# One-bank PSUM tiles in rotation for the last layer's FFN, and the norm product behind its first three blocks

## The chip, the core and the metric

The kernel runs on one core of a Trainium2 chip. TensorE (PE in the profile) does the matrix products and writes them into PSUM, 8 banks of 512 f32 in each of 128 partitions. VectorE (DVE), ScalarE (ACT) and GpSimd (POOL) work on tiles, and SyncE (SP) issues transfers. Each engine takes its instructions in the order of its program. The metric is the device time of one execution in microseconds. The kernel before takes 1583.85 us, the median of three runs (1581.45 to 1584.41).

## The reference, cut to what matters

One step of a decoder of two layers, for 512 prompt rows and 8 x 8 sample rows together (576 columns in the kernel, two halves of 288). The first layer mixes with attention, the second with a state-space layer and a GLU projection. After each mixer comes a feed-forward network (FFN) on the normed rows:

```
def rmsnorm(x, g):
    y = xf * lax.rsqrt(jnp.mean(xf * xf, axis=-1, keepdims=True) + RMS_EPS)
    return (y * g.astype(jnp.float32)).astype(x.dtype)
def swiglu(h, w_gate, w_up, w_down):
    return (jax.nn.silu(h @ w_gate) * (h @ w_up)) @ w_down
...
        h2 = rmsnorm(x, p['norm_ffn'][i])
        x = x + swiglu(h2, p['ffn_w_gate'][i], p['ffn_w_up'][i], p['ffn_w_down'][i]).astype(x.dtype)
```

The width is 1024, the FFN's inner width 2816. The step also returns the key and value caches, shifted by the new rows; these copies run beside everything else. The case is about the FFN of the second layer, the last part of the kernel.

## The kernel before

All of x lies transposed in SBUF (`xT`, 8 row blocks of 128 by 576 columns). Each f32 product is made of three matmuls on rounded values (type fp32r): weight and data are each split into a high and a low part (`whi`, `wlo`; `xoh`, `xol`), and high by high, high by low and low by high are added in PSUM.

**`ffn_last`** (from line 1098) works in 11 units of 256 columns of the inner width. In a unit (`unit`, from line 1138) the gate and the up product are formed together from seven products instead of eight, as in Strassen's way to multiply 2 x 2 blocks: `PRODUCTS` lists a11, s1, a12, s2, s3, a22, s4, each with the combination of the data that it takes. The data blocks are pairs of row blocks of x, so k = 0 to 3 counts four row pairs. `Norm7.add` (line 231) makes the data's combinations from each row pair as it is ready: by `put`, ScalarE writes the high and VectorE the low part. The weights' combinations s1, s3 and s4 are made by accumulating transfers that GpSimd issues (`plus`, L1123); s2 is an addition on VectorE (L1149), and s4 grows out of the tile of s2, in the buffers `S2`, shown as `S` in the profile.

Each of the seven products has two halves i of 128 output columns, and a half is 12 matmuls at L1160: four k by three splits. So a unit has 168. They go into three PSUM tiles X, Y and Z of two banks each, one bank for each half: X takes a11, s2, s3 and a22, one on top of the other, Y takes s1 and then s4, Z takes a12. Between these, copies of a bank are taken out: by ScalarE of a11 and s3 into `cp` (L1164), of s2 into `cq` (L1168), of a22 into `gt` or `ut` (L1170); by VectorE additions of a bank and a copy (L1166 at a12, L1172 at s4, L1174 behind s3). Then follow the norm's factor and silu (L1180, L1181), and the product split into `hh` and `hl` for the down product (L1186, L174, L175).

The weights of a product are split by ScalarE (`whi`, L1108) and VectorE (`wlo`, L1109) into three rotating buffers, so the split of one product waits until the product three before it is through.

After units 3, 7 and 10 (`THIRDS`) comes a group's down product: matmuls by `mm6` (L108), 384, 384 and 288 of them, into pairs of the same tiles. The first two groups scale by the norm's factor and add to `xT` (L1215, L1216), the last one, which has the factor already, adds at once (L1218), transposes the result on TensorE (L1226, L1227) and writes it out.

The norm's factor itself comes from `Norm.finish`: two matmuls by a matrix of ones (L203) sum the squares over the partitions, ScalarE takes Ln and Exp (L207, L209), VectorE refines. The squares are added up on GpSimd (L198). For the last FFN it stands ahead of `ffn_last`. The mixer's GLU projection before it ends with additions to `xT` (L1772, L1774), the last PSUM reads of that stage.

The order of the instructions on an engine is set by the framework's scheduler within the dependences, and the matmuls of the units are held in program order. A PSUM tile is tracked as a whole: who writes into any part of it waits for those who read any part of it before.

Of the kernel before, what the change touches and what calls it, by code (L numbers as in the profile page):

```python
# [8 lines left out]
F32 = mybir.dt.float32  # L9
# [10 lines left out]
T = 512  # L20
# [30 lines left out]
def _build(nc, tc, A, es):  # L51
# [104 lines left out]
    accp = [es.enter_context(tc.tile_pool(name=f"acc2{i}", bufs=1, space=PSUM)) for i in range(3)]  # L156
# [8 lines left out]
    aux = es.enter_context(tc.tile_pool(name="aux2", bufs=1, space=PSUM))  # L165
# [17 lines left out]
    class Norm:  # L183
# [16 lines left out]
        def finish(self):  # L200
            ps = aux.tile([128, 2, 512], F32, name="aux")
            for c in range(2):
                te.matmul(ps[:, c, :HN], ones, self.ss[:, c * HN:(c + 1) * HN], start=True, stop=True)  # L203
# [3 lines left out]
            s.activation(t, ps[:, :, :HN], AF.Ln, bias=eps, scale=1.0 / D)  # L207
            v.tensor_scalar(m, ps[:, :, :HN], -0.5 / D, -0.5 * EPS, op0=OP.mult, op1=OP.add)
            s.activation(self.r, t, AF.Exp, scale=-0.5)  # L209
            v.tensor_tensor(t, self.r, self.r, OP.mult)  # L210
            v.tensor_tensor(t, t, m, OP.mult)
            if self.perm:
                cs = lambda x: x.rearrange("p h x -> p (h x)").rearrange("p (c s) -> p c s", s=8)
                v.scalar_tensor_tensor(m.rearrange("p h x -> p (h x)").rearrange("p (s c) -> p c s", s=8), cs(t), 1.5, cs(self.r), op0=OP.add, op1=OP.mult)
                self.r = m
            else:
                v.scalar_tensor_tensor(self.r, t, 1.5, self.r, op0=OP.add, op1=OP.mult)

    class Norm7(Norm):
# [11 lines left out]
        def add(self, m):  # L231
            if m % 2 == 0:
                self.square(m)
                return
            j = m // 2
            ge, go = (gm[:, self.gi, k:k + 1] for k in (m - 1, m))
            e0, e1, o0, o1 = (xT[:, k, c * HN:(c + 1) * HN] for k in (m - 1, m) for c in range(2))
            t = self.tp.tile([128, 1024], F32, name="S2")
            a, b, c = (t[:, i * HN:(i + 1) * HN] for i in range(3))
            self.put("b11", j, e0, ge)  # L240
            s.activation(a, e1, AF.Copy, scale=ge)
            v.scalar_tensor_tensor(b, e0, ge, a, op0=OP.mult, op1=OP.subtract)
            self.put("t1", j, b, 1.0)
            self.put("b21", j, o0, go)
            v.scalar_tensor_tensor(c, o1, go, b, op0=OP.mult, op1=OP.add)
            self.put("t2", j, c, -1.0)
            v.scalar_tensor_tensor(a, o1, go, a, op0=OP.mult, op1=OP.subtract)
            self.put("t3", j, a, 1.0)
            v.scalar_tensor_tensor(b, o0, go, c, op0=OP.mult, op1=OP.subtract)
            self.put("t4", j, b, -1.0)  # L250
            self.put("b22", j, o1, go)
            self.square(m)
# [19 lines left out]
    n2.finish()  # L272
# [825 lines left out]
def ffn_last(nc, tc, A, L, nin, r7):  # L1098
    v, s, g, te = nc.vector, nc.scalar, nc.gpsimd, nc.tensor
    ident, pool, xT, ring, mm6, acc, accp, aux, pace, fetch_w = (L[x] for x in ("ident", "pool", "xT", "ring", "mm6", "acc", "accp", "aux", "pace", "fetch_w"))  # L1100
# [33 lines left out]
    with ExitStack() as es:  # L1134
        hp = es.enter_context(pool("hp", bufs=9))
        wk = es.enter_context(pool("wkf"))
        W = {0: fetch(0)}

        def unit(c, scaled):
            w = W.pop(c)  # L1140
            X, Y, Z = (accp[i].tile([128, 2, 512], F32, name=f"acc{i}") for i in range(3))
            bank = dict(a11=X, s1=Y, a12=Z, s2=X, s3=X, a22=X, s4=Y)
            cp = [[wk.tile([128, HN], F32, name=f"{n}{i}") for i in range(2)] for n in ("cp", "cq")]
            t = [[wk.tile([128, 2, HN], F32, name=f"{n}{m}") for m in range(2)] for n in ("gt", "ut")]
            sg = t[0]
            for n, x in PRODUCTS:
# [3 lines left out]
                wh, wl = split_w(w[n])  # L1150
# [5 lines left out]
                P = bank[n]  # L1156
                for i in range(2):
                    for k in range(4):
                        for j, (a, b) in enumerate(((wh, 0), (wh, 1), (wl, 0))):
                            tc.keep_in_program_order(te.matmul(P[:, i, :HN], a[:, k, i * 128:(i + 1) * 128], nin.x[x, k][b],  # L1160
                                                               skip_group_check=n not in ("a12",), start=n in ("a11", "s1", "a12") and k == 0 and j == 0, stop=n in ("a12", "a22", "s4") and k == 3 and j == 2))
                    p = P[:, i, :HN]
                    if n in ("a11", "s3"):
                        s.activation(cp[0][i], p, AF.Copy)  # L1164
                    elif n == "a12":
                        v.tensor_tensor(t[i][0][:, 0], p, cp[0][i], OP.add)  # L1166
                    elif n == "s2":
                        s.activation(cp[1][i], p, AF.Copy)  # L1168
                    elif n == "a22":
                        s.activation(t[i][1][:, 0], p, AF.Copy)  # L1170
                    elif n == "s4":
                        v.tensor_tensor(t[i][0][:, 1], p, cp[1][i], OP.add)  # L1172
                    if n == "s3":
                        v.tensor_tensor(t[i][1][:, 1], Y[:, i, :HN], cp[0][i], OP.add)  # L1174
                    m = {"a22": 1, "s4": 0}.get(n)
                    if m is None:
                        continue
                    sgn = -1.0 if m else 1.0
                    if i == 0:
                        v.scalar_tensor_tensor(sg[m], sg[m], sgn, nin.r, op0=OP.mult, op1=OP.mult)  # L1180
                        s.activation(sg[m], sg[m], AF.Silu)  # L1181
                        if scaled:
                            g.tensor_tensor(sg[m], sg[m], nin.r, OP.mult)
                    else:
                        u = t[1][m]
                        v.scalar_tensor_tensor(u, u, sgn, sg[m], op0=OP.mult, op1=OP.mult)  # L1186
                        h[2 * c + m] = L["split"](hp, u.rearrange("p a b -> p (a b)"), None, "hh", "hl")

        for c0, c1 in THIRDS:
# [5 lines left out]
            for c in range(4):  # L1195
                ps = [acc() for _ in range(3 if scaled and c == 3 else 2)]
                ws = []
                for a in range(0, len(ks), 4):
                    n = min(4, len(ks) - a)
                    ws.append(split_w(fetch_w(dram(A["ffn_w_down"], D * FF, [[1, D * FF]]), D, ks[a], n, c * 256, 256, 1.0)))  # L1200
                    if scaled and c == 3:
                        continue
                    for m in range(2):
                        for k in range(n):
                            wh, wl = (x[:, k, m * 128:(m + 1) * 128] for x in ws[-1])
                            mm6(ps[m], wh, wl, *h[ks[a + k]], a + k == 0, a + k == len(ks) - 1)
                for m in range(2):
                    if scaled and c == 3:
                        for a, k in enumerate(ks):
                            wh, wl = (w[:, a % 4, m * 128:(m + 1) * 128] for w in ws[a // 4])  # L1210
                            mm6(ps[m], wh, wl, *h[k], a == 0, k == ks[-1])
                    xv = xT[:, 2 * c + m, :].rearrange("p (a b) -> p a b", a=2)
                    if not scaled:
                        y = wk.tile([128, 2, HN], F32, name=f"gt{m}")
                        v.tensor_tensor(y, ps[m][:, :, :HN], nin.r, OP.mult)  # L1215
                        v.tensor_tensor(xv, y, xv, OP.add)  # L1216
                        continue
                    v.tensor_tensor(xv, ps[m][:, :, :HN], xv, OP.add)  # L1218
# [5 lines left out]
                    pt = ps[2] if c == 3 and m else aux.tile([128, 2, 512], F32, name="aux")  # L1224
                    for b in range(4):
                        te.transpose(pt[:, 0, b * 128:(b + 1) * 128], xT[:, 2 * c + m, b * 128:(b + 1) * 128], ident)  # L1226
                    te.transpose(pt[:64, 1, :128], xT[:, 2 * c + m, T:], ident)  # L1227
                    s.activation(yo[:, :, o:o + 128], pt[:, 0, :].rearrange("p (b f) -> p b f", b=4), AF.Copy)
                    v.tensor_copy(ys[:, o:o + 128], pt[:64, 1, :128])
# [621 lines left out]
```

## Time and profile before

| | |
|---|---|
| median of three runs | 1583.85 us (1581.45 to 1584.41) |
| profiled execution | 1578.9 us, of which the span of the profile is 1577.1 us |
| PE busy | 1456.6 us, 92% of the span |
| DVE, ACT, POOL busy | 1002.3, 600.3, 333.7 us |
| L1160, the three splits' matmuls | 616 each, mean 311, 297 and 297 ns |
| clock granted to TensorE over the span | 0.99 |

A line of the profile names the source line, the engine, the operation, the output and the inputs; then how often, the busy time and the mean duration in ns; then how long the engine stood idle just before, and which instruction ended that. Line numbers up to about 200 belong to helpers that several stages share. A busy time of TensorE is not pure work: the end of a matmul is modelled, and each is shown to overlap the next. The last FFN takes the time from about 1063.5 us to the end.

### The profile page before, as it was taken

The numbers are of one execution on the slowest core, as the hardware profiler recorded it, in microseconds if no ns is written. First come the engines' busy times: TensorE is split into PE (matmuls) and PEld (weight loads), VectorE is DVE, ScalarE is ACT, GpSimd is POOL, SyncE is SP. The second block draws the span as 40 slices with busy tenths as digits, with TensorE's granted clock in tenths as the row PEclk, the third lists the DMA queues.
The fourth block names the chain that finished last, engine by engine and source line by source line (L and its number), as shares of the span: only waits on it lengthen the run. The fifth ranks groups of instructions, "written<-read, shape, count | busy, mean of one in ns | idle before, by whom it ended". The sixth has DMA issues, their size and how long they took to land.

```text
span 1577.1 us, 30037 instructions
## 1 busy us (share of the span) xinstructions
PE 1456.6 (92%) x12398; PEld 1348.2 (85%) x12398; DVE 1002.3 (64%) x1669; ACT 600.3 (38%) x959; POOL 333.7 (21%) x410
## 2 busy tenths in 40 slices
PE   9999999999999999999999979996778977798788
PEld 7888777677999999999999979995778976798678
DVE  5898898544787447786866685756544455444542
ACT  4535555555622212222225444434433234322332
POOL 2012233200210661634452112111000000000110
PEclk9999999999999999999999989999999999999999
DMA  7576889999967676988887596424556555655232
GB/s 257 191 269 201 280 262 311 336 318 309 311 238 282 240 270 242 340 313 298 300 281 277 178 282 180 134 93 107 124 139 230 186 136 132 173 186 130 72 96 64
DMA packets 181048, 345.73 MB, mean 219 GB/s; under 512 B 40720, under 2 KB 116304, under 8 KB 179504
## 3 DMA queue, kind: packets, MB, share of 16 engines
q1 hardware_dynamic: 168176, 309.00, 57.2%
q0 software_dynamic: 9968, 32.12, 9.1%
q10 hardware_dynamic: 2768, 2.70, 0.5%
q8 instruction: 97, 1.59, 0.4%
q14 instruction: 39, 0.32, 0.1%
HBM read 312.29 MB, written 118.78 MB: 273 GB/s over the span
## 4 chain that ended last, share of the span: by engine, by line
PE 77%; DVE 6%; ACT 6%; issue 4%; DMA 4%; POOL 3%; SPq 0%; ACTq 0%; DVEq 0%; POOLq 0%
PE acc L108 41%; PE acc L1160 14%; PE acc L380 12%; ACT whi L1108 2%; PE Sd L807 2%; DMA kc<-cache_kv_w 1%; PE O L807 1%; PE S L807 1%; PE pt L613 1%; DMA U<-u_scr 1%; PE aux L108 1%; ACT cp L1164 1%; DVE ut L1186 1%; DVE wlo L1109 1%; PE pt L807 1%
## 5 line engine op out<-in xcount | busy, mean ns | idle before, releaser
L1160 PE MATMUL acc<-xoh,whi 128*128 128x288 f32 x616 | 191.5, 311 | 78.1 <-ACT cp L1164 28.0
L108 PE MATMUL acc<-xgh,wlo 128*128 128x288 f32 x1056 | 227.7, 297 | 3.8 <-DVE wlo L100 3.8
L108 PE MATMUL acc<-xgh,whi 128*128 128x288 f32 x1056 | 229.7, 299 | 0.0
L108 PE MATMUL acc<-xgl,whi 128*128 128x288 f32 x1056 | 227.5, 297 | 0.0
L1160 PEld LDWEIGHTS acc<-xoh,whi 128*128 128x128 f32 x616 | 116.9, 190 | 97.3 <-ACT cp L1164 35.4
L99 ACT ACTIVATE whi<-raw 128x1024 fp32r<-128x1024 f32 x98 | 102.0, 1041 | 243.1 <-PE acc L108 191.7
L1160 PE MATMUL acc<-xol,whi 128*128 128x288 f32 x616 | 182.9, 297 | 0.0
L1160 PE MATMUL acc<-xoh,wlo 128*128 128x288 f32 x616 | 182.7, 297 | 0.0
L108 PEld LDWEIGHTS acc<-xgh,wlo 128*128 128x128 f32 x1056 | 170.6, 189 | 4.4 <-DVE wlo L100 4.2
L108 PEld LDWEIGHTS acc<-xgh,whi 128*128 128x128 f32 x1056 | 170.4, 189 | 1.8 <-issue 1.2
L108 PEld LDWEIGHTS acc<-xgl,whi 128*128 128x128 f32 x1056 | 170.6, 189 | 0.1
L100 DVE TENSOR_TENSOR wlo<-raw,whi 128x1024 fp32r<-128x1024 f32 x98 | 125.8, 1283 | 67.2 <-ACT whi L99 65.9
L108 PE MATMUL acc<-hh,whi 128*128 128x288 f32 x704 | 152.3, 297 | 5.0 <-ACT whi L1108 3.1
L108 PE MATMUL acc<-hh,wlo 128*128 128x288 f32 x704 | 151.2, 296 | 0.2 <-DVE wlo L1109 0.2
L108 PE MATMUL acc<-hl,whi 128*128 128x288 f32 x704 | 151.2, 296 | 0.0
L1109 DVE TENSOR_TENSOR wlo<-raw,whi 128x1024 fp32r<-128x1024 f32 (+1 forms) x57 | 67.7, 1188 | 93.0 <-ACT whi L1108 92.9
L380 PE MATMUL acc<-whi,xh 128*128 128x512 f32 x288 | 118.7, 414 | 0.5 <-ACT xh L320 0.4
L108 PEld LDWEIGHTS acc<-hh,whi 128*128 128x128 f32 x704 | 112.8, 188 | 7.1 <-ACT whi L1108 3.8
L1160 PEld LDWEIGHTS acc<-xol,whi 128*128 128x128 f32 x616 | 117.0, 190 | 0.1
L1160 PEld LDWEIGHTS acc<-xoh,wlo 128*128 128x128 f32 x616 | 117.1, 190 | 0.0
L1108 ACT ACTIVATE whi<-raw 128x1024 fp32r<-128x1024 f32 (+1 forms) x57 | 58.7, 1030 | 152.4 <-PE acc L1160 69.7
L108 PEld LDWEIGHTS acc<-hh,wlo 128*128 128x128 f32 x704 | 113.1, 188 | 0.4 <-DVE wlo L1109 0.4
(441 smaller groups left out, 2824.1 us busy)
## 6 DMA issues: line engine op xcount, KB each, us to landing
o_kv_s<-cache_kv_w SPq DMA_DIRECT2D x64, 1020.0 KB, 7.8
kc<-cache_kv_w SPq DMA_DIRECT2D x100, 512.0 KB, 6.7
raw<-ffn_w_down SPq DMA_DIRECT2D x40, 512.0 KB, 4.0
raw<-w_qkv SPq DMA_DIRECT2D x36, 512.0 KB, 7.1
raw<-w_gu SPq DMA_DIRECT2D x33, 512.0 KB, 3.3
kc<-qscr SPq DMA_DIRECT2D x32, 512.0 KB, 6.1
o_kv_s<-cache_kv_w SPq DMA_DIRECT2D x16, 1008.0 KB, 7.4
raw<-ffn_w_gate SPq DMA_DIRECT2D x22, 512.0 KB, 5.9
```

The source lines that it names most:

```text
L99: s.activation(hi, raw, AF.Copy)
L100: mark[0] = v.tensor_tensor(lo, raw, hi.bitcast(F32), OP.subtract)
L108: pem[0] = te.matmul(ps[:, c, :HN], w, x[:, c * HN:(c + 1) * HN], start=first and i == 0, stop=last and i == 2)
L380: ins = nc.tensor.matmul(*a, **kw)
L613: tc.keep_in_program_order(te.transpose(kp[:, hp, :], self.kc[u // 2][:, u % 2, hp * 128:(hp + 1) * 128], ident))
L807: return lambda *a, **kw: self.tc.keep_in_program_order(f(*a, **kw))
L1108: s.activation(hi, raw, AF.Copy)
L1109: v.tensor_tensor(lo, raw, hi.bitcast(F32), OP.subtract)
L1160: tc.keep_in_program_order(te.matmul(P[:, i, :HN], a[:, k, i * 128:(i + 1) * 128], nin.x[x, k][b], skip_group_check=n not in ("a12",), sta ...
L1164: s.activation(cp[0][i], p, AF.Copy)
L1186: v.scalar_tensor_tensor(u, u, sgn, sg[m], op0=OP.mult, op1=OP.mult)
```

## The change

All accumulating PSUM pools of the stages before are closed ahead of `ffn_last`, which opens one pool of its own: eight tiles of one bank, handed out in rotation. Each half of a product has a tile to itself, so X, Y and Z become six tiles a unit; the down products take four tiles for each 256 output columns, the transposes two each. Operations that read two banks at once (Ln and the norm's scaling in `finish`, the scaling and addition behind the down products) become two operations of half the size.

In unit 0 the first three products run over k = 0 to 2 first, 54 matmuls, and then over k = 3, 18 matmuls. `finish` stands behind them. `Norm7.add` no longer waits for the second row block of a pair before it makes b11 and t1, which need only the first, and takes the square last.

```
+        bk = es.enter_context(tc.tile_pool(name="bk", bufs=8, space=PSUM))
+        bank = lambda: bk.tile([128, 512], F32, name="bank")
...
-            X, Y, Z = (accp[i].tile([128, 2, 512], F32, name=f"acc{i}") for i in range(3))
-            bank = dict(a11=X, s1=Y, a12=Z, s2=X, s3=X, a22=X, s4=Y)
+            acc = {}
...
+            def products(n, x, i, ks):
+                q = dict(a11="x", s2="x", s3="x", a22="x", s1="y", s4="y", a12="z")[n], i
+                if q not in acc:
+                    acc[q] = bank()
+                wh, wl = hl[n]
+                for k in ks:
+                    for j, (a, b) in enumerate(((wh, 0), (wh, 1), (wl, 0))):
+                        tc.keep_in_program_order(te.matmul(acc[q][:, :HN], a[:, k, i * 128:(i + 1) * 128], nin.x[x, k][b], skip_group_check=n != "a12",
+                                                           start=n in ("a11", "s1", "a12") and k == 0 and j == 0, stop=n in ("a12", "a22", "s4") and k == 3 and j == 2))
+                if 3 in ks:
+                    ended(n, i, acc[q][:, :HN])
...
+            rest = PRODUCTS
+            if c == 0:
+                rest = PRODUCTS[3:]
+                for ks in (range(3), (3,)):
+                    for n, x in PRODUCTS[:3]:
+                        if ks != (3,):
+                            ready(n)
+                        for i in range(2):
+                            products(n, x, i, ks)
+                nin.finish([bank(), bank()])
...
-                ps = [acc() for _ in range(3 if scaled and c == 3 else 2)]
+                ps = [[bank(), bank()] for _ in range(2)]
...
-    n2.finish()
+    pss.close()
     ffn_last(nc, tc, A, L, n2, sp["ring"])
```

`ready` does the split of a product's weights, `ended` what was done at the end of a half before. In the changed kernel the matmuls of the units stand at L1171, `finish` at L206 and its following lines, the transposes at L1262 and L1263, the down products' matmuls at L1234.

TensorE at the start of unit 0, before: the last matmul of the GLU projection (L108), the norm's product (L203), and the first matmul of the units, into tile X.

```order
L108 MATMUL acc_12480<-xgh,wlo 128x288 x2
L203 MATMUL aux<-ssum,ones 128x288 [waits Pool_49]
L203 MATMUL aux<-ssum,ones 128x288
L1160 MATMUL acc_12667<-xoh,whi 128x288 [waits DMAHW3_49,DMAHW2_49,DMAHW4_49,DMAHW1_49,DMAHW5_49,DMAHW0_49,DMAHW6_49,DMASW7_49,DMAHW7_49,DVE_49,Activation_49]
L1160 MATMUL acc_12667<-xol,whi 128x288
```

And in the changed kernel, from the same place to behind the 72 matmuls of the first three products:

```order
L108 MATMUL acc_12484<-xgh,wlo 128x288 x2
L1171 MATMUL bank<-xoh,whi 128x288 [waits DMAHW3_49,DMAHW2_49,DMAHW4_49,DMAHW1_49,DMAHW5_49,DMAHW0_49,DMAHW6_49,DMASW7_49,DMAHW7_49,DVE_49,Activation_49]
L1171 MATMUL bank<-xol,whi 128x288
...
L1171 MATMUL bank<-xoh,wlo_12723 128x288
L206 MATMUL bank<-ssum,ones 128x288 [waits Pool_49]
L206 MATMUL bank<-ssum,ones 128x288
L1171 MATMUL bank<-xoh,whi 128x288 [waits Activation_49]
```

The norm's product has moved behind 72 matmuls, and with it the wait for GpSimd's sum of squares; the last row is the first matmul of s2.

TensorE in a later unit, from the first half of s2 to the second of s4, only the rows with which a half begins, before. The number behind a name tells tiles apart: `acc0` is X, `acc1` is Y.

```order
L1160 MATMUL acc0_15611<-xoh_11771,whi_15712 128x288 [waits Activation_49]
...
L1160 MATMUL acc0_15611<-xoh_11776,whi_15743 128x288 [waits Activation_49]
...
L1160 MATMUL acc0_15611<-xoh_11781,whi3_15787 128x288 [waits Activation_49]
...
L1160 MATMUL acc1_15612<-xoh_11785,whi_15825 128x288 [waits DVE_49]
...
L1160 MATMUL acc1_15612<-xoh_11785,whi_15825 128x288 [waits DVE_49]
```

The same in the changed kernel:

```order
L1171 MATMUL bank_15693<-xoh_11775,whi_15785 128x288 [waits Activation_49]
...
L1171 MATMUL bank_15707<-xoh_11775,whi_15785 128x288 [waits Activation_49]
...
L1171 MATMUL bank_15693<-xoh_11780,whi_15816 128x288 [waits Activation_49]
...
L1171 MATMUL bank_15707<-xoh_11780,whi_15816 128x288 [waits Activation_49]
...
L1171 MATMUL bank_15725<-xoh_11789,whi_15898 128x288 [waits DVE_49]
...
L1171 MATMUL bank_15738<-xoh_11789,whi_15898 128x288 [waits DVE_49]
```

The order of the products is the same. Both halves went into one tile; now they alternate between two, and the wait in each row is for the reader of that tile alone. On ScalarE the copy of the second half of s2 (`cq1`) stands behind the split of s4's weights (`whi<-S2`) in both kernels, and so does the copy of s3's second half (`cp1`) behind the next unit's first split; here the changed kernel:

```order
L1182 ACTIVATE cq0_15683<-bank_15693 128x288 [waits PE_49]
L1112 ACTIVATE whi_15898<-S2_15783 128x1024 [waits DMASW3_49,DVE_49,PE_49]
L1182 ACTIVATE cq1_15684<-bank_15707 128x288 [waits PE_49]
L1178 ACTIVATE cp0_15681<-bank_15693 128x288 [waits DVE_49,PE_49]
L1112 ACTIVATE whi_15944<-raw_15820 128x1024 [waits DMAHW4_49,PE_49,Activation_49]
L1178 ACTIVATE cp1_15682<-bank_15707 128x288 [waits DVE_49,PE_49]
```

TensorE in the last group, before: the transposes of one row block (L1226, L1227) stand among the matmuls of a later block.

```order
L108 MATMUL acc2_16683<-hl_16112,whi_16688 128x288
L1226 MATMUL aux_16664<-ident_63,xT_5020 128x128 [waits DVE_49,Activation_49]
L1226 MATMUL aux_16664<-ident_63,xT_5020 128x128 x3
L1227 MATMUL aux_16664<-ident_63,xT_5020 64x128
L108 MATMUL acc2_16683<-hl_16112,whi_16688 128x288
```

In the changed kernel they stand right behind the last matmul of their own block:

```order
L1234 MATMUL bank_16781<-hh_16392,wlo_16793 128x288
L1262 MATMUL bank_16836<-ident_63,xT_5020 128x128 [waits DVE_49]
L1262 MATMUL bank_16836<-ident_63,xT_5020 128x128
L1262 MATMUL bank_16836<-ident_63,xT_5020 128x128 [waits DVE_49]
L1262 MATMUL bank_16836<-ident_63,xT_5020 128x128
L1263 MATMUL bank_16837<-ident_63,xT_5020 64x128
L1234 MATMUL bank_16782<-hh_15932,whi_16786 128x288
```

The two waits on VectorE are for the two halves of the addition to `xT`, which reads the block's last matmuls.

More of the change, by code (lines that the diff above doesn't have):

```diff
@@ L198, in square, with finish @@
                 g.tensor_tensor(self.ss, self.ss, sq, OP.add)
[L200 to L201 removed]
+        def finish(self, two=None):
+            if two is None:
+                ps = aux.tile([128, 2, 512], F32, name="aux")
+                two = [ps[:, c] for c in range(2)]
             for c in range(2):
[L203 removed]
+                te.matmul(two[c][:, :HN], ones, self.ss[:, c * HN:(c + 1) * HN], start=True, stop=True)
             self.r = nrm.tile([128, 2, HN], F32, name="rstd")
@@ L1155, in unit @@
                     W[c + 1] = fetch(c + 1)
-                P = bank[n]
-                for i in range(2):
[L1158 to L1187, printed above, removed]
```

123 lines of the change are left out of this document (80 added, 43 removed).

## The prediction

> **What bounds the kernel now.** I read the page's chain and groups first. The group's row gives a line's operation, tiles, number, then busy time and mean ns, then the idle time of TensorE just before it and who ended most of it.
>
> ```profile
> PE acc L108 41%; PE acc L1160 14%; PE acc L380 12%; ACT whi L1108 2%; PE Sd L807 2%; DMA kc<-cache_kv_w 1%; PE O L807 1%; PE S L807 1%; PE pt L613 1%; DMA U<-u_scr 1%; PE aux L108 1%; ACT cp L1164 1%; DVE ut L1186 1%; DVE wlo L1109 1%; PE pt L807 1%
> L1160 PE MATMUL acc<-xoh,whi 128*128 128x288 f32 x616 | 191.5, 311 | 78.1 <-ACT cp L1164 28.0
> ```
>
> The end is a chain of matmuls. In the changed stage, the gate and up products at L1160, TensorE stands idle 78.1 us ahead of them, and the work that ends this is not a load of weights but a copy out of PSUM. Where those waits lie shows in the matmuls of one unit (TensorE's timeline, 1284 to 1317.8 us, only rows with idle time ahead; in brackets that time and what ended it):
>
> ```profile
> 1283.63 0.40 PE L1160 MATMUL acc<-xoh,whi 128*128 128x288 f32 x1 [1.73 <-DVE gt L1172]
> 1287.91 0.40 PE L1160 MATMUL acc<-xoh,whi 128*128 128x288 f32 x1 [0.84 <-ACT cp L1164]
> 1295.61 0.40 PE L1160 MATMUL acc<-xoh,whi 128*128 128x288 f32 x1 [1.06 <-DVE gt L1166]
> 1299.56 0.41 PE L1160 MATMUL acc<-xoh,whi 128*128 128x288 f32 x1 [0.50 <-ACT cq L1168]
> 1302.73 0.40 PE L1160 MATMUL acc<-xoh,whi 128*128 128x288 f32 x1 [1.31 <-ACT cq L1168]
> 1305.09 0.40 PE L1160 MATMUL acc<-xoh,whi 128*128 128x288 f32 x1 [0.50 <-ACT cp L1164]
> 1308.31 0.40 PE L1160 MATMUL acc<-xoh,whi 128*128 128x288 f32 x1 [1.36 <-ACT cp L1164]
> 1310.67 0.40 PE L1160 MATMUL acc<-xoh,whi 128*128 128x288 f32 x1 [0.50 <-ACT gt L1170]
> 1315.83 0.40 PE L1160 MATMUL acc<-xoh,whi 128*128 128x288 f32 x1 [1.73 <-DVE gt L1172]
> ```
>
> From one `gt L1172` wait to the next is 32.20 us. Eight waits idle 7.80 us in it. They cost more than that, because a matmul's shown 0.29 us overlaps the next one's. Without a wait matmuls start 0.1326 us apart, by the first and last of 20 in a row:
>
> ```profile
> 1100.26 0.29 PE L1160 MATMUL acc<-xol,whi 128*128 128x288 f32 x1
> ...
> 1102.78 0.29 PE L1160 MATMUL acc<-xoh,wlo 128*128 128x288 f32 x1
> ```
>
> A unit's 168 matmuls need 22.3 us, so 9.9 us of its 32.2 are lost. The table by stage (length, then busy time of each engine, TensorE's clock, DMA share, GB/s) shows how often that is paid. The rows are unit 0 with what precedes it, units 1 and 2, unit 3 with the first group's down products, units 4 to 6, unit 7 with its group, units 8 and 9, and unit 10 with the last group:
>
> ```profile
> 1063.50:1106.50 43.00, 27.73 (x170) 25.18 (x171) 27.05 (x35) 21.14 (x32) 5.37 (x5) 0.91 0.42 111
> 1106.50:1139.87 33.37, 25.91 (x172) 24.03 (x171) 16.48 (x20) 13.00 (x19) 2.60 (x3) 0.96 0.53 126
> 1139.87:1172.05 32.18, 24.38 (x170) 22.52 (x170) 16.47 (x20) 12.89 (x19) 2.60 (x3) 1.00 0.53 131
> 1172.05:1253.47 81.42, 75.43 (x554) 73.56 (x554) 38.14 (x45) 22.01 (x29) 2.88 (x4) 1.00 0.63 206
> 1253.47:1285.20 31.73, 24.26 (x170) 22.39 (x169) 16.10 (x19) 12.25 (x18) 2.31 (x3) 1.00 0.54 133
> 1285.20:1317.40 32.20, 24.40 (x171) 22.52 (x170) 16.47 (x20) 12.88 (x19) 2.60 (x3) 1.00 0.53 130
> 1317.40:1349.60 32.20, 24.40 (x171) 22.53 (x170) 16.47 (x20) 12.89 (x19) 2.60 (x3) 1.00 0.53 131
> 1349.60:1432.40 82.80, 75.70 (x556) 73.61 (x555) 38.15 (x45) 22.15 (x29) 2.99 (x4) 1.00 0.56 176
> 1432.40:1464.10 31.70, 24.23 (x170) 22.37 (x169) 16.10 (x19) 12.23 (x18) 3.67 (x5) 1.00 0.49 116
> 1464.10:1498.00 33.90, 24.46 (x171) 22.59 (x170) 16.61 (x20) 12.88 (x19) 3.75 (x4) 1.00 0.30 84
> 1498.00:1571.00 73.00, 66.69 (x493) 64.61 (x491) 29.14 (x42) 21.94 (x33) 5.15 (x4) 1.00 0.26 78
> ```
>
> VectorE is busy 16.5 us of a unit, ScalarE 12.9, the DMA engines 0.53 x 32.2 = 17.1. All lie under 22.3: without its waits, TensorE is the bound.
>
> **The change, part by part.** *One bank per half, middle units.* Before, both halves of a product share one tile, and a matmul into one half waits for the copy out of the other. Now a half's matmul waits only for its own half's copy, made 12 matmuls (1.59 us) earlier or more. Both halves of a11, s1, a12 and s4 find banks that were read long ago, so the waits of 0.84, 1.06 and 1.73 us go wholly. For s2 to s3 and s3 to a22 the copy of the second half stays behind a split on ScalarE:
>
> ```profile
> 1289.67 1.06 ACT L1108 ACTIVATE whi<-S 128x1024 fp32r<-128x1024 f32 x1 [1.82 <-PE acc L1160]
> ...
> 1301.32 1.06 ACT L1108 ACTIVATE whi<-S 128x1024 fp32r<-128x1024 f32 x1 [1.82 <-PE acc L1160]
> 1302.28 0.39 ACT L1168 ACTIVATE cq<-acc 128x288 f32<-128x288 f32 x1
> ```
>
> The matmul at 1299.56 begins 12, which without waits would be followed at about 1301.3; the next came at 1302.73, 1.5 us later. This delay now lies under the other half's 1.59 us: 0.1 us to spare, likewise for a22 (1306.8 against 1308.31). I allow 0.3 us a unit for so thin a cover and take 22.6 us. Nothing else in the unit gets shorter; its eight transfers of 512 KB simply come faster.
>
> Units 1, 2, 4, 5, 6, 8, 9: 227.3 us by their rows, 7 x 22.6 = 158.2 after. Gain 69.1.
>
> *The S transfer.* The accumulating transfer that makes s4 starts when `wlo` of s2 is split, and s4's own split needs it:
>
> ```profile
> 1292.29 0.86 POOL L1123 DMA_DIRECT2D S<-w_gu  x1 [5.01 <-DVE wlo L1109]
> DMA to landing us min/median/max: 5.3/5.4/6.3
> ```
>
> The issue comes 2.62 us after the split of s2 (1289.67), which follows a11's 24 matmuls (3.2 us): 5.9 us into the unit. It lands at 11.3 by the middle duration, at 12.2 by the longest, ahead of the 12.8 us at which s2 ends and s4's split can begin. The slack is 0.6 to 1.5 us. If it goes, ScalarE waits in order, the second half's `cq` behind it, and s3's second half on TensorE behind that. Cost taken: nothing.
>
> *The start.* The norm's product stood ahead of unit 0's first matmul; now 54 matmuls that need only three row pairs come first (rows of TensorE, VectorE, ScalarE and TensorE again).
>
> ```profile
> 1070.06 2.29 PE L203 MATMUL aux<-ssum,ones 128*128 128x288 f32 x4 [6.59 <-POOL ssum L198]
> 1064.97 0.74 DVE L1772 TENSOR_TENSOR yt<-acc,yt 128x576 f32<-128x576 f32 x1
> 1072.52 1.28 ACT L207 ACT_TABLE_LOAD   x1
> 1073.82 0.74 ACT L207 ACTIVATE sq<-aux,eps 128x576 f32<-128x576 f32 x1
> 1084.58 0.40 PE L1160 MATMUL acc<-xoh,whi 128*128 128x288 f32 x1 [1.05 <-DVE gt L1166]
> ```
>
> The first matmul must still wait for the last tile out of the old PSUM pools (`yt`), now behind less of VectorE's work: about 1064.9, 1.4 us into the first window. Then: 72 matmuls 9.5; 0.5 until the last rows' operands are there; the norm's product 1.2 (half its 2.29, which it took at half clock, 0.51 in the row below); 96 matmuls 12.7. ScalarE's Ln, Exp and two table loads, some 4.1 us, now stand among the copies of s2 and s3, which fill about 2 us more: 6 in 6.4 us. I charge 2.4 us of waiting. Sum 27.7 against 43.00. Gain 15.3. If this cover failed wholly, the 4.1 us would be paid instead of 2.4.
>
> Of the clock: it fell to half twice here, after the 6.59 us of idling, and in a stretch where TensorE was 65% busy and idled 1.80 us at most:
>
> ```profile
> 1068.40:1075.30 6.90, 5.17 (x16) 4.25 (x16) 6.58 (x11) 4.49 (x7) 1.53 (x1) 0.51 0.00 0
> 1104.88 0.40 PE L1160 MATMUL acc<-xoh,whi 128*128 128x288 f32 x1 [1.80 <-DVE gt L1172]
> 1105.90:1109.30 3.40, 3.40 (x17) 3.40 (x16) 2.30 (x4) 2.17 (x3) 0.86 (x1) 0.51 0.37 75
> ```
>
> One more such stretch would cost half of 3.4 us, 1.7; I keep it in the range only, since waits shrink. The Trainium skill ("TensorE: Matmul & The Clock Gate", section "What's actually happening") has the clock fall to half after at least one idle window of some 3.4 us. By that rule the 1.4 us here would never drop it and the 1.7 us is zero; the second stretch in the trace, with no such idle time ahead, disagrees, so I don't rely on it.
>
> *Groups.* Unit 3's row holds 168 + 384 matmuls, 73.2 us, of its 81.42; unit 7's the same of 82.80. I leave 1.5 us in each, since the first weights of the down product are now wanted sooner: 6.7 + 8.1 gained. Unit 10's row holds 168 + 288 and about 3.7 us of transposes, 64.2 of 73.00. The transposes now stand directly behind the additions they read, which are cut in halves:
>
> ```profile
> 1565.12 0.76 DVE L1218 TENSOR_TENSOR xT<-acc,xT 128x576 f32<-128x576 f32 x1 [1.83 <-PE acc L108]
> 1285.52 0.46 DVE L1172 TENSOR_TENSOR ut<-acc,cq 128x288 f32<-128x288 f32 x1 [0.48 <-PE acc L1160]
> ```
>
> A half takes 0.46 us as here, with the way there and back some 0.7 to 0.9. Before, nearly 30 matmuls of the next product hid that; now it is open four times, partly under the first half's transposes: 2.5 us. With 1.5 as above the row becomes 68.2; gain 4.8.
>
> Splitting Ln and the scaling by halves in the two earlier norms adds two operations each, beside other products: nothing, at worst 0.4 us each.
>
> *Sum.* 69.1 + 15.3 + 6.7 + 8.1 + 4.8 = 104.0. The profiled execution took 1578.9 us (span 1577.1), 4.95 under the median of 1583.85. It becomes 1474.9; by the median 1479.9, so **1480 us**.
>
> **Rivals.** *The S transfers land late.* With twice the transfers per time they may take as long as the longest accumulating transfer into the s tiles, 10.0 us:
>
> ```profile
> DMA to landing us min/median/max: 2.4/4.8/10.0
> ```
>
> They decide from 6.9 us on. At 10.0 each of 11 units waits 3.1 us: 34 more, 1514. Against it: S itself never took over 6.3 us, and the down stage moves 206 GB/s where a unit of 22.6 us needs 4.2 MB, 186 GB/s. Chance 0.12.
>
> *The copies come too late.* If the 0.1 us margins fail, the two places keep what a short wait costs now, 0.50 idle plus 0.27 of restarting: 1.5 us a unit, 17 in 11 units, 1497. For it: ScalarE's order is unchanged; against it: the delays of 1.5 us are measured with their split in them. Chance 0.10.
>
> *The waits stay.* If the dependence on the neighbouring half were not by tile, or closing the old pools held up the start by what it saves, the time stays near 1583. Against it: at 1312 a22's second half and s4's first follow each other without wait, in different tiles. Chance 0.03.
>
> *Transfers become the bound.* The DMA engines' 17.1 us per unit would stretch if loads and accumulating transfers hinder each other when packed. At 1.3 times they reach 22.3; at 1.9, 32.2, and the unit gains nothing; past 2.0 the start's gain is used up. At 2.1 a unit takes 35.9: 11 x 3.7 = 41 lost, 15 gained, 1609. Against it: the stage at 206 GB/s keeps 0.63 share, which is no more share per GB/s. Chance 0.03.
>
> **How the numbers follow.** The forecast has 0.72. Its own range: down to 1470 if the 0.3, 1.5 and 2.4 us are mostly not paid; up to 1492 if they double. To hold 8 in 10 the range takes in the late copies and the late S transfers: 1470 to 1515. What a measurement of this kernel can tell from no change is about 0.2%, 3 us. All but the last two rivals are faster: 0.94; the waits that stay, 0.03 the same; 0.03 slower.
>
> **What would show it.** Right: the units' rows fall to 22.3 to 23 us, all idle rows inside a unit vanish but for traces of `cq` and `cp`; the products of unit 0 start within 2 us of the last matmul of the mixer's projection, and its s2 follows the norm's product some 12 us after that; the transposes show four waits on VectorE. Wrong: units of 24 to 26 us with waits on `cq` behind a split that waits on S (late transfers), or with 0.5 us waits on both copies (margin), waits on `whi` before the down products over 2 us, or units still of 32 us.

## The result and the profile after

The changed kernel takes 1473.79 us, the median of four runs (1470.25 to 1481.82), against 1582.65 us for the kernel before in the same runs: a ratio of 0.9324 with a 95% interval of 0.928 to 0.9369. The prediction said 1480 us, with 1470 to 1515. The profiled execution took 1472.93 us, with a span of 1471.1. One later execution of the changed kernel ran in a slow state, at a mean clock of 0.654, and took 1977.07 us; it is left out of every time below.

To compare stretches of two traces I count from the start of the last matmul of the GLU projection, since what precedes it varies by some us from run to run. The two rows, before and after (in such a row stand the start, the length, the engine, the line, the operation and its tiles):

```profile
1063.03 0.43 PE L108 MATMUL acc<-xgh,wlo 128*128 128x288 f32 x2
1065.05 0.43 PE L108 MATMUL acc<-xgh,wlo 128*128 128x288 f32 x2
```

I call these starts the mark, and the stretch from there to the end the tail. It is 514.07 us before and 406.05 after. The whole gain, 108.0 us, lies in the last FFN; what precedes it took 2.0 us longer in the trace after.

The group of the page that answers to L1160 before, with its idle time of 78.1 us:

```profile
L1171 PE MATMUL bank<-xoh,whi 128*128 128x288 f32 x616 | 182.5, 296 | 4.2 <-ACT cq L1182 2.8
```

TensorE now stands idle 4.2 us ahead of these matmuls in all. By stage (length, busy time of PE, PEld, DVE, ACT, POOL, then TensorE's clock, DMA share, GB/s) the rows that answer to unit 0, unit 1, unit 3 with its group, unit 6, unit 7 with its group, and unit 10 with the last group to the last addition:

```profile
1065.30:1091.90 26.60, 24.36 (x173) 23.11 (x172) 23.54 (x33) 19.40 (x31) 5.51 (x5) 1.00 0.56 147
1091.90:1114.80 22.90, 22.52 (x170) 22.27 (x169) 16.51 (x22) 12.84 (x20) 2.60 (x3) 1.00 0.77 198
...
1137.70:1211.50 73.80, 73.80 (x555) 73.45 (x554) 40.10 (x55) 22.82 (x31) 2.79 (x4) 1.00 0.72 234
...
1256.90:1279.30 22.40, 22.40 (x171) 22.39 (x170) 16.01 (x21) 12.43 (x19) 2.59 (x3) 1.00 0.76 189
1279.30:1352.90 73.60, 73.49 (x554) 73.26 (x553) 39.92 (x55) 22.78 (x31) 2.59 (x3) 1.00 0.66 205
...
1398.50:1465.30 66.80, 66.15 (x494) 64.19 (x492) 33.35 (x53) 22.93 (x35) 6.30 (x5) 1.00 0.30 90
```

In unit 6 PE is busy for the whole of its 22.40 us: there is nothing left to gain but the matmuls themselves. The units not shown (2, 4, 5, 8 and 9) took 22.9, 22.3, 23.1, 22.4 and 23.2 us. The clock is 1.00 in every row, unit 0 included.

What waits are left, on TensorE's timeline (rows with idle time ahead, from unit 0 and 1 and from the end):

```profile
1066.84 0.37 PE L1171 MATMUL bank<-xoh,whi 128*128 128x288 f32 x1 [1.36 <-ACT sq L198]
...
1081.68 0.40 PE L1171 MATMUL bank<-xoh,whi 128*128 128x288 f32 x1 [0.26 <-ACT cq L1182]
1083.97 0.40 PE L1171 MATMUL bank<-xoh,whi 128*128 128x288 f32 x1 [0.44 <-ACT cq L1182]
...
1106.88 0.40 PE L1171 MATMUL bank<-xoh,whi 128*128 128x288 f32 x1 [0.38 <-ACT cq L1182]
...
1459.65 0.81 PE L1262 MATMUL bank<-ident,xT 128*128 128x128 f32 x4 [0.42 <-DVE xT L1254]
1465.77 0.80 PE L1262 MATMUL bank<-ident,xT 128*128 128x128 f32 x4 [0.41 <-DVE xT L1254]
```

The first row names a square on ScalarE as releaser, but what ended last there is VectorE's reading of the old pools, 0.1 us ahead of the matmul:

```profile
1065.99 0.75 DVE L1808 TENSOR_TENSOR yt<-acc,yt 128x576 f32<-128x576 f32 x1
```

But for 0.19 us in unit 0, where a weight's low part was late, the waits on `cq` are the only ones inside the units. One of them, at 1106.88 in unit 1, goes back to the transfer into S (rows of GpSimd, then of ScalarE):

```profile
1096.71 0.87 POOL L1127 DMA_DIRECT2D s<-w_gu  x1 [10.12 <-DVE ut L1200]
1098.01 0.86 POOL L1127 DMA_DIRECT2D S<-w_gu  x1 [0.44 <-DVE wlo L1113]
...
1105.47 1.06 ACT L1112 ACTIVATE whi<-S 128x1024 fp32r<-128x1024 f32 x1 [1.70 <-DMA S<-w_gu]
1106.43 0.39 ACT L1182 ACTIVATE cq<-bank 128x288 f32<-128x288 f32 x1
```

The split of S waits 1.70 us for the transfer, the copy of s2's second half stands behind the split, and the matmul at 1106.88 behind the copy. Over the 11 units of this trace:

```profile
DMA to landing us min/median/max: 5.4/6.0/7.8
```

### The profile page after: what moved, and what is told of

The parts are those of the page before. It is cut to its first block, busy times and chain, and to the rows that moved or that the text cites. A ratio compares the mean times of both kernels' runs of the same rounds, so it can differ in the third digit from the quotient of the medians.

```text
span 1471.1 us, 30038 instructions
## 1 busy us (share of the span) xinstructions
PE 1432.1 (97%) x12398; PEld 1341.1 (91%) x12398; DVE 1000.9 (68%) x1696; ACT 596.0 (41%) x962; POOL 334.6 (23%) x410
## 5 line engine op out<-in xcount | busy, mean ns | idle before, releaser
L108 PE MATMUL acc<-xgh,wlo 128*128 128x288 f32 x1056 | 227.6, 297 | 3.4 <-DVE wlo L100 3.4
L108 PE MATMUL acc<-xgh,whi 128*128 128x288 f32 x1056 | 229.5, 299 | 0.0
L108 PE MATMUL acc<-xgl,whi 128*128 128x288 f32 x1056 | 227.3, 297 | 0.0
L1171 PE MATMUL bank<-xoh,whi 128*128 128x288 f32 x616 | 182.5, 296 | 4.2 <-ACT cq L1182 2.8
L1171 PE MATMUL bank<-xoh,wlo 128*128 128x288 f32 x616 | 181.7, 295 | 0.2 <-DVE wlo L1113 0.2
L1171 PE MATMUL bank<-xol,whi 128*128 128x288 f32 x616 | 181.7, 295 | 0.0
L108 PEld LDWEIGHTS acc<-xgh,wlo 128*128 128x128 f32 x1056 | 170.6, 189 | 4.0 <-DVE wlo L100 3.9
L108 PEld LDWEIGHTS acc<-xgh,whi 128*128 128x128 f32 x1056 | 170.3, 189 | 1.8 <-issue 1.2
L108 PEld LDWEIGHTS acc<-xgl,whi 128*128 128x128 f32 x1056 | 170.5, 189 | 0.1
L1171 PEld LDWEIGHTS bank<-xoh,whi 128*128 128x128 f32 x616 | 115.7, 188 | 6.1 <-ACT cq L1182 4.4
L1171 PEld LDWEIGHTS bank<-xoh,wlo 128*128 128x128 f32 x616 | 115.8, 188 | 0.6 <-DVE wlo L1113 0.6
L1171 PEld LDWEIGHTS bank<-xol,whi 128*128 128x128 f32 x616 | 115.7, 188 | 0.1
L384 PE MATMUL acc<-wlo,xh 128*128 128x512 f32 x288 | 112.2, 391 | 0.0
L384 PE MATMUL acc<-whi,xl 128*128 128x512 f32 x288 | 111.5, 393 | 0.0
L108 PE MATMUL acc<-hh,whi 128*128 128x288 f32 x352 | 76.2, 297 | 0.0
L1080 POOL TENSOR_TENSOR gt<-gt,rstd 128x576 f32<-128x576 f32 x22 | 39.4, 1794 | 160.5 <-ACT gt L1079 160.4
```

What stands on the lines that cost most here:

```text
L108: pem[0] = te.matmul(ps[:, c, :HN], w, x[:, c * HN:(c + 1) * HN], start=first and i == 0, stop=last and i == 2)
L384: ins = nc.tensor.matmul(*a, **kw)
L1080: g.tensor_tensor(t, t, nin.r, OP.mult)
L1171: tc.keep_in_program_order(te.matmul(acc[q][:, :HN], a[:, k, i * 128:(i + 1) * 128], nin.x[x, k][b], skip_group_check=n != "a12", start=n ...
```

## The experiments

All are one edit away from the changed kernel or from each other. Theory: the gain is the waits of one half for the other half's copy, which go because each half has its own tile. First rival: it is the start, where the norm's product no longer stands in the way. All but two of the runs below are single executions, so I go by the tails and the rows of their traces rather than by their times.

**Two banks to a tile.**

```
-        bk = es.enter_context(tc.tile_pool(name="bk", bufs=8, space=PSUM))
-        bank = lambda: bk.tile([128, 512], F32, name="bank")
+        bk = es.enter_context(tc.tile_pool(name="bk", bufs=4, space=PSUM))
+        pair = []
+        def bank():
+            if not pair:
+                both = bk.tile([128, 2, 512], F32, name="bank")
+                pair.extend((both[:, 0], both[:, 1]))
+            return pair.pop(0)
```

> The changed kernel with one thing undone: the two halves of a product share a tile of two banks again (four such tiles in rotation); the early start stays. Theory (the gain sits in the halves that no longer wait for each other's copies): the units go back to 32.2 us from 22.3 to 23.2, with the same idle rows ahead of eight halves; some 9.4 us in each of ten units and about 8 in unit 0, so 1570 to 1576 us and a profiled execution of some 1572. Rival (the gain sits in the start and in the closing of the old pools, and the rotation of more tiles lifts the waits by itself): units of 22 to 25 us, under 1500.

Measured: 1579.98 us beside 1584.04 for the kernel before; tail 513.6 us, against 514.07 before the change. The windows of unit 0 and unit 2:

```profile
1065.00:1107.70 42.70, 29.55 (x171) 26.89 (x171) 26.44 (x36) 20.86 (x33) 5.57 (x5) 0.87 0.41 111
...
1140.00:1172.20 32.20, 24.39 (x170) 22.53 (x169) 16.49 (x21) 12.88 (x19) 2.60 (x3) 1.00 0.53 131
```

The 32.20 us are back, and with them the eight idle rows (in unit 2: 0.84, 1.06, 0.50, 1.31, 0.50, 1.36, 0.50 and 1.73 us, the very figures from before the change). It went further than expected: the start brought nothing either. Where its gain went shows on GpSimd, ScalarE and TensorE in unit 0:

```profile
1080.59 0.88 POOL L1127 DMA_DIRECT2D s<-w_gu  x1 [9.57 <-DVE ut L1187]
1081.16 1.21 POOL L1127 DMA_DIRECT2D S<-w_gu  x1
...
1091.51 1.06 ACT L1112 ACTIVATE whi<-S 128x1024 fp32r<-128x1024 f32 x1 [4.50 <-DMA S<-w_gu]
...
1092.92 0.40 PE L1178 MATMUL bank<-xoh,whi 128*128 128x288 f32 x1 [3.99 <-ACT cp L1185]
```

The two accumulating transfers were issued 0.57 us apart, and S landed after 10.3 us.

**The norm's product ahead again**, with one-bank tiles:

```
             if c == 0:
-                rest = PRODUCTS[3:]
...
-                nin.finish([bank(), bank()])
+                nin.finish([bank(), bank()])
```

> The changed kernel with the norm's product ahead of unit 0 again and its first three products over all four row pairs in one go; the one-bank tiles stay. Theory (the place of the norm's product gives some 7 of the 16 us that the start gained, the tiles the rest): from the last matmul of the GLU projection to the first of s2 it takes 12.3 us in the changed kernel and should take 18 to 21 here, with some 6.4 us idle ahead of the norm's product and a stretch at half clock behind; the two waits on cq in unit 0 (0.26 and 0.44 us idle) go; in all 5 to 9 us slower, 1479 to 1483. Rival (the tiles give all of the start's gain): 0 to 1 us slower.

Measured: 1487.2 us, tail 419.8, 13.7 more than the changed kernel, 11.8 of it ahead of unit 1. Two waits make up most of that, each with matmuls at half clock behind it (their lengths of 2.29 and 0.61 us show it):

```profile
1071.89 2.29 PE L206 MATMUL bank<-ssum,ones 128*128 128x288 f32 x4 [5.83 <-POOL ssum L199]
1094.34 0.61 PE L1171 MATMUL bank<-xoh,whi 128*128 128x288 f32 x1 [5.51 <-ACT cq L1182]
```

The first was expected. The second wasn't: S was issued 0.57 us behind another accumulating transfer again and landed after 9.7 us. So more was lost than by the place alone, and the size is not settled by this run; the run further down, without that transfer, does it.

**No split over row pairs**, `for ks in (range(3), (3,))` made `for ks in (range(4),)`:

> The changed kernel, but the first three products of unit 0 run over all four row pairs in one go, and the norm's product stays behind them. The difference is only whether they are begun with three of four row pairs. Theory, from the changed kernel's trace: the operands of the fourth pair that a11 and s1 need come out of the row block before the last and are ready by 1070.2, ahead of 1071.6 when s1 would reach them, and those of a12 by 1072.7, ahead of 1074.8; so nothing waits and the time is the same within 0.5 us. Rival (the split over row pairs carries the early start): a wait of 2 to 6 us inside the first 72 matmuls.

And the same with `Norm7.add` as it was before the change:

> As the run without the split over row pairs, and the operands of a row pair are made all at once again, when its second row block is written (the square first). Theory (the scheduler puts ScalarE's and VectorE's operations where their inputs are ready, whatever the order in the code): the same within 1 us, the square of 0.7 us ahead of the first operand being the only difference. Rival (split and order are each other's safety net, and one of the two is needed): a11's last three matmuls of a half wait for operands made behind the last row block, 2 to 4 us more than without the split alone.

Measured: 1472.32 and 1474.97 us; tails 409.5 and 408.8, where the changed kernel has 406.1 and, run again, 408.2. In neither is there a wait for operands inside the first 72 matmuls. But with the old `add` the first of them starts 2.8 us behind the mark instead of 1.8: VectorE's last reading of the old pools ends 1.0 us later there, behind the making of a low part that took 1.34 us instead of 0.52. Both runs lost time in unit 0 at another place, some 1.6 us in the run without the split:

```profile
1079.24 0.40 PE L1171 MATMUL bank<-xoh,whi 128*128 128x288 f32 x1 [1.96 <-ACT cq L1182]
```

and on ScalarE just before it:

```profile
1076.91 1.28 ACT L213 ACT_TABLE_LOAD   x1
1078.20 0.68 ACT L213 ACTIVATE rstd<-sq 128x576 f32<-128x576 f32 x1
1078.79 0.39 ACT L1182 ACTIVATE cq<-bank 128x288 f32<-128x288 f32 x1
```

The scheduler put `cq` behind both table loads instead of between them. Beginning with three of four row pairs is not what lets TensorE start; the operands of the fourth pair are in time either way. Against the changed kernel's two traces, which differ by 2.1 us themselves, the two runs are 0.6 to 3.4 us slower. The run without the split lost still more in unit 2, 3.2 us beyond the same unit of the changed kernel, where the edit changes nothing: S landed after 9.1 us, and the clock was 0.50 for 3.4 us behind the wait (rows of GpSimd and TensorE):

```profile
1117.79 0.86 POOL L1127 DMA_DIRECT2D S<-w_gu  x1 [2.14 <-DVE wlo L1113]
...
1128.42 0.40 PE L1171 MATMUL bank<-xoh,whi 128*128 128x288 f32 x1 [2.02 <-ACT cq L1182]
```

**s4 on VectorE.** The suspected wait taken away, with the work done elsewhere:

```
-                    plus(w["s4"], c, 0, 1)
+                    v.tensor_tensor(w["s4"], w["s2"], w["a12"], OP.add)
```

> The changed kernel with s4 made by an addition on VectorE (the tile of s2 plus the loaded tile of a12) in place of the accumulating transfer into S. In the changed kernel that transfer lands 5.4 to 7.8 us after its issue, and in units 1, 2, 5 and 9 TensorE waits for cq behind it, about 3 us in all. Theory (these waits are the late transfer's): no wait on cq in units 1 to 10 and the units at 22.3 to 22.5 us; 2 to 4 us faster than the changed kernel. Rival (the copy behind a split of 1.06 us is late by itself, or VectorE's 1.23 us more a unit is felt): the waits on cq stay within 0.3 us of what they are, no gain.

> The changed kernel once more, beside the others on the same chip: 1470 to 1482 us as before. By either theory it is the base for the run with s4 on VectorE, which should be 2 to 4 us under it or equal to it.

Measured: 1467.82 us with a ratio of 0.9301 (0.9287 to 0.9314), and 1472.78 us with 0.9323 (0.9307 to 0.9339) for the changed kernel beside it. The two intervals overlap, so the timing alone doesn't settle it; the traces do, with tails of 403.9 against 406.1 and 408.2. Units 1 and 2 with s4 on VectorE (windows that begin 0.8 us ahead of the units):

```profile
1089.00:1111.30 22.30, 22.30 (x170) 22.28 (x169) 17.72 (x23) 14.30 (x21) 1.70 (x2) 1.00 0.69 185
1111.30:1133.60 22.30, 22.30 (x170) 22.27 (x169) 17.00 (x22) 12.44 (x19) 1.71 (x2) 1.00 0.62 166
```

From unit 1 on no matmul of the units waits for anything. So the copies behind a split were in time; the waits on `cq` were the late transfer's. Of the kernels here this is the fastest.

**s1 on VectorE**, to find out why S is late; S stays a transfer:

```
-            plus(w[n], c, *a)
+            if n == "s3":
+                plus(w[n], c, *a)
...
+        v.tensor_tensor(w["s1"], w["s1"], w["a22"], OP.add)
```

> The changed kernel with s1 made by an addition on VectorE (its loaded tile plus the loaded tile of a22) in place of the accumulating transfer into s that is issued 1.3 to 2.9 us ahead of S; S stays a transfer. Theory (S lands late where it meets that other accumulating transfer: 5.4 us when it is issued 5.3 us or more behind one, 6.0 to 7.8 when 1.3 to 2.9 behind): S lands at 5.0 to 5.7 us in units 1 to 10, and the waits on cq go. Rival (S lands late for the load of all transfers, which come faster in shorter units): S still takes over 6 us in half of the units.

Measured: 1470.17 us, tail 405.1. S landed after 5.1 to 5.3 us in units 0 to 9:

```profile
DMA to landing us min/median/max: 5.1/5.2/7.4
```

The 7.4 is unit 10, and cost a wait of 2.00 us on `cq`; there no other accumulating transfer was near, nor was one when the changed kernel's second trace had 7.7 us at the same place. For units 1 to 9 the theory holds, for unit 10 the cause is open. The edit takes one of a unit's eight transfers away altogether; whether a plain transfer at the same place would hold S up as well isn't shown.

**S issued twice:**

```
                     plus(w["s4"], c, 0, 1)
+                    plus(w["s4"], c, 0, 1)
```

> The changed kernel with the accumulating transfer into S issued twice, one behind the other, so that s4 holds a12 twice: the suspected wait doubled. Theory (S decides from 6.9 us behind its issue on, and each us later costs one a unit): it is ready some 12 to 14 us after the issue of the first, 5 to 7 us late, in 11 units: 50 to 75 us slower, 1525 to 1550. Rival (split buffers and ScalarE's queue have more slack than reckoned): under 20 us slower.

Measured: 1561.47 us, tail 496.4, 90 us more: 8.2 a unit. The unit that ends its wait at 1150.84 has S split at 1149.44, 14.4 us after the first issue, 7.5 later than the 6.9 at which it decides. TensorE shows 5.62 us of idle time, and a second price around and behind it (the row's window: length, PE, PEld, DVE, ACT, POOL, clock):

```profile
1150.84 0.61 PE L1172 MATMUL bank<-xoh,whi 128*128 128x288 f32 x1 [5.62 <-ACT cp L1179]
```

```profile
1150.80:1154.20 3.40, 3.36 (x14) 3.36 (x15) 3.40 (x4) 1.31 (x3) 0.00 (x0) 0.50 0.06 11
1154.20:1157.60 3.40, 3.40 (x19) 3.40 (x19) 1.22 (x3) 1.20 (x2) 0.00 (x0) 0.65 0.43 154
```

The clock is halved for 5.7 us behind the wait: the last 48 matmuls of the unit take 9.0 us where they need 6.4, so about 2.7 more, and the unit becomes 30.7 us long. The idle times of the 11 units sum to 67 us, inside the expected range; that the whole came out above it is mostly the price of the slower matmuls behind each wait.

**The norm's product ahead, s4 on VectorE:** both edits from above.

> One-bank tiles, the norm's product ahead of unit 0 and no split over row pairs, and s4 made on VectorE: the run with the norm's product ahead, without its late transfer into S. That run lost 13.7 us against the changed kernel from the last matmul of the GLU projection to the end, of which 5.5 were a wait for S in unit 0. Theory (the place of the norm's product is worth the idle time ahead of it and the half clock behind it, 5 to 7 us): the stretch from the start of the last GLU matmul to the end, 403.9 us with s4 on VectorE and the norm's product behind, becomes 409 to 412. Rival (the 13.7 us are all of the norm's place, the wait for S only stands where another would): 416 or more.

Measured: 1477.21 us, tail 409.26 against 403.95: the place of the norm's product is worth 5.3 us, of which 4.5 lie ahead of unit 1. s2 starts 7.1 us later than with the norm's product behind, and the rest of unit 0 gets 2.5 us of that back, since TensorE waits for no copy there. The rows of the idle time and of the clock behind it:

```profile
1072.18 2.29 PE L206 MATMUL bank<-ssum,ones 128*128 128x288 f32 x4 [5.85 <-POOL ssum L199]
```

```profile
1072.00:1076.00 4.00, 3.82 (x12) 3.25 (x13) 4.00 (x9) 3.07 (x6) 0.13 (x1) 0.50 0.00 0
```

**X alone shared**, with s4 on VectorE:

```
+        bx = es.enter_context(tc.tile_pool(name="bx", bufs=1, space=PSUM))
...
+                if q == ("x", 0):
+                    if q not in acc:
+                        both = bx.tile([128, 2, 512], F32, name="both")
+                        acc["x", 0], acc["x", 1] = both[:, 0], both[:, 1]
```

> The run with s4 on VectorE, but the halves of a11, s2, s3 and a22 share one tile of two banks again (X), while the halves of s1, s4 and a12 keep a tile each. Theory (the waits of a unit add up wait by wait): the six idle rows of X come back, 5.0 us of idle time plus 0.27 of restarting each, so 6.6 a unit: units of 28.9 us. Rival (with X shared the others return too, or one wait hides the next): units of 31 us and more, or of 26 and less.

Measured: 1540.11 us, tail 476.8. A unit, from the wait of s2's second half to the next unit's:

```profile
1108.45 0.40 PE L1176 MATMUL both<-xoh,whi 128*128 128x288 f32 x1 [0.50 <-ACT cq L1187]
...
1137.39 0.40 PE L1176 MATMUL both<-xoh,whi 128*128 128x288 f32 x1 [0.50 <-ACT cq L1187]
```

That is 28.94 us, with six waits in it. Their idle times sum to 5.08 us; with 0.27 us of restarting each and the 22.3 us of the matmuls that makes 29.0. The waits add up one by one.

**Two banks to a tile, s4 on VectorE:**

> The run with tiles of two banks and the early start, with s4 made on VectorE. With two banks the last FFN took as long as before the change although the norm's product stood behind 72 matmuls; in unit 0 the transfer into S, issued 0.57 us behind another accumulating one, landed after 10.3 us and TensorE waited 3.99 us behind it. Theory (that one late transfer ate the start's gain): unit 0, with what precedes it from the last GLU matmul on, becomes 38 to 39.5 us where it was 42.7, the later units stay at 32.2. Rival (the shared tiles and ScalarE's table loads eat it by themselves): 41.5 us or more.

Measured: 1573.34 us, tail 507.4. The mark and the first matmul of unit 1:

```profile
1064.25 0.43 PE L108 MATMUL acc<-xgh,wlo 128*128 128x288 f32 x2
...
1102.29 0.29 PE L1178 MATMUL bank<-xoh,whi 128*128 128x288 f32 x1
```

That is 38.0 us, against 43.7 with the transfer (1064.60 to 1108.27) and 44.0 before the change (1063.03 to 1107.04). So with shared tiles the early start is worth some 6 us, and the late S of unit 0 ate nearly all of it. By the tails, all but some 7 us of the changed kernel's gain needs the one-bank tiles.

## Why the prediction came out right

*The waits per unit.* Right in mechanism. 7 x 22.6 = 158.2 us were predicted for the seven middle units, 159.2 measured. The three runs with shared tiles show the cause: what is shared waits, wait by wait, and what is not doesn't. That the size fits within 1.0 us is partly luck: the 0.3 us a unit held back for thin cover, 2.1 in all, was not needed, and the transfer into S, charged at nothing, took some 3 us.

*The thin margins at s3 and a22.* The 0.1 us held. Without the late S no unit waits at all, so the rival by which these copies come too late falls.

*The S transfer.* Here a step failed, a small one. I took its landing from a trace in which it was issued 5.8 us or more behind the other accumulating transfer nearly everywhere, up to 6.3 us, and concluded that there was slack. In shorter units that other transfer, for s1, moved to 1.3 to 2.9 us ahead of S, and S took 6.0 to 7.8 us, over the 6.9 at which it decides in four units, three of which then waited. Together with unit 9, where S landed in 5.4 us but was issued 8 us into the unit, this cost some 3 us (four waits of 2.1 us in all, and their restarting), not the 34 of that rival. The rival had the place right and the size wrong, and the cause I gave in it, twice the transfers per time, is not the main one for units 1 to 9, since without the accumulation of s1 it landed at 5.1 to 5.3 us while the unit's other transfers came as fast. A hint stood in the trace before: the longest of its landings there, 6.3 us, belongs to the one S that was issued 1.71 us behind another.

*The start.* 27.7 us predicted, 26.6 measured. But the sum was made of two edits under one heading, and the heading, the place of the norm's product, is the smaller part: 4.5 us of unit 0, 5.3 of the tail, with one-bank tiles. The rest of the 16.4 us is mainly unit 0's share of the waits between halves: with the norm's product left ahead and s4 on VectorE, the tiles alone bring the stretch from the mark to unit 1 from 44.0 to 32.4 us. The 2.4 us charged for Ln, Exp and table loads among the copies were 0.7 idle and 0.5 of restarting in the end.

*The clock.* The 1.7 us held in the range were not paid. The trace after has no stretch at half clock in the last FFN until its last microsecond. With no idle time over 1.4 us left, this trace agrees with the Trainium skill's one idle window of some 3.4 us ("TensorE: Matmul & The Clock Gate", section "What's actually happening"). Other traces don't: the second stretch in the trace before stays unexplained by it, and half clock stood behind waits of 1.96 us (old `add`), 2.02 (no split) and 2.62 and 2.99 us (the two runs with two-bank tiles), all shorter than such a window. So it was right not to rely on it.

*Groups and end.* The 1.5 us held back for the first weights of each down product were not needed: 73.8 and 73.6 us measured, 74.7 predicted. The transposes wait twice, 0.42 and 0.41 us, not four times: under the transposes of the first half the second one's addition is hidden but for 0.1 us. The last row came to 66.8 instead of 68.2.

In all 4 us more were gained than the 104.0 of the sum: 1.1 at the start, 2.0 in the groups, 1.4 at the end, less 1.0 in the units, and half a us in the short stretches ahead of the first window and behind the last. The rest of the distance from 1480 to 1473.79 lies in the medians, which scatter by some us from run to run.

## What to carry to other kernels

Where a wait is tracked by tile, a tile that holds two independent accumulators makes each wait for the other's reader; count those waits in the trace, with the restart behind each, before looking for faster operations. A transfer's slack read from a slow schedule doesn't hold in a faster one: ask which other transfers will then stand next to it. When two edits are made together, their sum can be right while their shares are not; only runs with one of them undone tell.

## What the runs showed of the hardware that was not expected

An accumulating transfer of 512 KB lands later when another one was issued shortly before it. Over all traces in which S is a single transfer, it landed after 5.0 to 6.0 us when no other was issued in the 5 us ahead (but for unit 10, 5.3 to 7.7), after 5.7 to 9.1 us when one was issued 1.3 to 3.2 us ahead, and after 9.7 and 10.3 us at 0.57 us. Where S was issued twice, the second one took 5.6 to 11.4 us in units 1 to 10, although the first had landed 0.3 us before its issue; that doesn't fit, and stays open. What the second one waits for the traces don't show.

A wait of TensorE can cost twice, as idle time and then as a stretch at half clock: 2.7 us more behind 5.62. In the last FFN of these traces such a stretch, of 3.4, 6.8 or 10.2 us, lies around or behind each of the 19 waits of 2.6 us and more. Behind waits of about 2 us it came in some cases (2.02 us in the run without the split) and not in others (2.00 us in the run with s1 on VectorE); the traces don't show what decides.
